# Expert lookups for eight tokens a visit, marks of 2048 elements, and three conditioning tiles moved

## The chip, the cores and the metric

The kernel runs on one core of one Trainium2 chip. The metric is the device time of one execution in microseconds (us); several runs of a kernel are taken, and their median counts. The engines are PE (matmuls; its weight loads are shown as PEld), DVE (elementwise and reductions), ACT (activations and copies), POOL, and SP, which here only issues DMA transfers. Each works through its own queue in order, and semaphores make one wait for another.

## What is computed

A chain of three transformer blocks on 256 tokens of width 1024: a first one with two attention mixers, a second one with two attentions and a gated feed-forward, and a third one that is conditioned on a vector c and ends in a mixture of many small experts. The change lies in the third, cut here to what matters:

```python
c_act = silu(c)
mod = c_act @ w_ada[l] + b_ada[l]            # 6 * 1024 conditioning values
shift1, scale1, gate1, shift2, scale2, gate2 = split(mod, 6)
h = modulate(x, norm_mix_g[l], shift1, scale1)
...                                          # pooling and attention, x = x + gate1 * ...
h2 = modulate(x, norm_ffn_g[l], shift2, scale2)
x = x + gate2 * peer_ffn(h2, ...)

def peer_ffn(h, w_q, sub_keys, u_tab, v_tab):
    # 8 heads: the 16 best of 128 keys on each of two sides, then the 16 best pairs:
    # expert = i * 128 + j out of 16384, with a softmax weight g
    u, vv = u_tab[expert], v_tab[expert]
    a = gelu(einsum('cd,chkd->chk', x, u))
    return einsum('chk,chkd->cd', g * a, vv)
```

## The kernel before

Activations are kept transposed, 128 features on the partitions and the 256 tokens along the row. Weights are streamed: `Weights` (lines 207 to 251) has one list of tiles of 128x1024 (512 KB), in the order in which they are used. A tile `wraw` is loaded by SP (L225, four buffers, three loads ahead). For precision it is split in two: `whi` by ACT (L242) and `wlo` by DVE (L243), and each projection step makes three matmuls, `whi` with the high part of the activations `hxh` (L460), `whi` with the low part `hxl` (L461), `wlo` with `hxh` (L462). There are three buffers for a split pair, and the split runs two tiles ahead of the matmuls.

The conditioning row `mod` is made on the side. Its 48 tiles of `w_ada` are put into the same list between others, at places given by the table `ADA`; such a tile is not split, but multiplied by silu(c) and summed along the row by one operation on DVE (L302, with a short read of the sum). So a conditioning tile costs one load in SP's queue, one of the four `wraw` buffers, and one place in DVE's queue. The names in the table are the weights after whose tiles they stand: `b2_ffn` the feed-forward of block two, `b3_v`, `b3_qk`, `b3_u`, `b3_g`, `b3_br` the values, queries and keys, pooling input, gates and branch products of block three, `pv` the experts' second table.

At the end of block two's feed-forward DVE makes `ft` from the gate (L1182, L1183), ACT and DVE split it into `fah` (L1186) and `fal` (L1187), PE multiplies by the last rows (L1173 to L1175) into the banks `s` and `t`, DVE adds to `xT` (L1047), and PE sums over `xT` (L431) for the norm. In block three attention is woven between the projections (`weave`, with a rate: so much of the side work for each step of the main work). A branch chunk's result in bank `pj` is taken over by DVE (L1329 `rx`, L1331 `sp`).

The experts (`peer`): routing finds each token's 128 pairs (i, j) and weights g. Then the products of all 16384 experts are made as a dense projection of 128 tiles (`u_evac`), and at the same time the table of weights `a[i, token]` is built from lookups (`combine`), woven in at the rate R_PEER. For one token a one-hot matrix of its keys i, times a one-hot matrix of its keys j scaled by g, gives a 128x128 table of weights: two matmuls of 128 columns (the weights g are in two parts of 16 bits). DVE makes the two matrices, called marks here: `ohx` (L1536, a comparison with a row of numbers) and `ohy` (L1539, `ohx` of the other key times g), for four tokens in one operation, two buffers each. One visit of PE (L1556) makes the eight matmuls of four tokens into one of the two PSUM banks `o`. Then DVE (L1566) and ACT (L1570) evacuate the bank: what of `a` already holds its product is multiplied by DVE, the rest is only written by ACT, and the later products are multiplied in by L1517. R_PEER, OHCOST and EVCOST say how much of this is due for each step of the projection. The final order of each engine's queue is set by the framework's scheduler from the order of writing.

## Time and profile before

| | us |
|---|---|
| median of three runs (1666.72 to 1670.72) | 1669.85 |
| the profiled execution, its own time | 1667.41 |
| its span, first to last instruction | 1665.6 |
| PE busy | 1618.2 (97%) |
| DVE busy | 1239.2 (74%) |
| ACT busy | 955.8 (57%) |
| first and last visit's lookups on PE | 981.3 and 1282.2 |

A row of a timeline gives the start, the duration, engine, line, operation, output and inputs with their shapes, a count of merged rows, and in brackets the idle time before it and who ended that. Matmuls overlap, so what a matmul costs is the distance between two starts, not the duration in its row. In a table of stretches each engine has its busy time in the stretch, with the number of instructions; PEclk is the granted share of TensorE's full clock.

### The profile page before, as it was taken

What the parts mean: (1) busy time and instruction counts of PE and PEld (TensorE: products, weight loads), DVE (VectorE), ACT (ScalarE), POOL (GpSimd) and SP (SyncE); (2) the same over time, 40 slices, a digit from 0 to 9 for tenths busy, and PEclk for the clock granted to TensorE, in tenths of its full rate; (3) what the DMA queues carried; (4) which work ended last, traced back from release to release, by engine and by line L of the source; (5) the groups of instructions that cost most, each with busy time, mean ns of one, the idle gap of its engine ahead of it and who ended that gap; (6) DMA issues with size and microseconds to landing.
All of it is one profiled execution on the core that took longest, in us unless ns stands there. A gap on an engine that the chain in (4) does not pass through costs nothing.

```text
span 1665.6 us, 30998 instructions
## 1 busy us (share of the span) xinstructions
PE 1618.2 (97%) x11828; PEld 1482.4 (89%) x11828; DVE 1239.2 (74%) x2502; ACT 955.8 (57%) x1810; POOL 182.1 (11%) x198
## 2 busy tenths in 40 slices
PE   9999999999999999999999999999999999999997
PEld 7999887788889999789989899999999888888886
DVE  6887888776776666787768987778887566666565
ACT  6775577568755555566555455555444655555554
POOL 2000234430120000111037000000000000000000
PEclk9999999999999999999999999999999999999999
DMA  7444552275247777447755555555555666666663
GB/s 253 146 138 149 170 184 79 84 226 161 90 129 252 245 236 254 150 143 228 259 160 169 164 190 172 170 165 172 168 168 170 199 222 213 214 213 209 185 195 115
DMA packets 84229, 300.07 MB, mean 180 GB/s; under 512 B 10288, under 2 KB 11184, under 8 KB 83824
## 3 DMA queue, kind: packets, MB, share of 16 engines
q1 hardware_dynamic: 83360, 295.90, 55.9%
q10 hardware_dynamic: 720, 2.19, 0.4%
q8 instruction: 93, 1.52, 0.4%
q14 instruction: 56, 0.46, 0.1%
HBM read 296.07 MB, written 1.05 MB: 178 GB/s over the span
## 4 chain that ended last, share of the span: by engine, by line
PE 69%; DVE 11%; DMA 7%; ACT 5%; issue 4%; POOL 1%; SPq 0%; POOLq 0%; DVEq 0%; ACTq 0%
PE s L1598 10%; PE t L1598 10%; PE pj L460 7%; PE pj L461 7%; PE pj L462 7%; DMA wraw<-in_ada 6%; DVE wlo L243 5%; PE s L460 3%; PE s L461 3%; PE t L460 3%; PE s L462 3%; PE t L461 3%; PE t L462 3%; PE o L607 2%; PE o L1556 2%
## 5 line engine op out<-in xcount | busy, mean ns | idle before, releaser
L242 ACT CAST whi<-wraw 128x1024 fp32r<-128x1024 f32 x504 | 528.9, 1051 | 356.0 <-PE pj L461 105.7
L243 DVE TENSOR_TENSOR wlo<-wraw,whi 128x1024 fp32r<-128x1024 f32 x486 | 598.9, 1238 | 172.8 <-ACT whi L242 170.7
L460 PE MATMUL pj<-hxh,whi 128*128 128x256 f32 x1448 | 412.1, 285 | 2.7 <-ACT hxh L1161 1.2
L461 PE MATMUL pj<-hxl,whi 128*128 128x256 f32 x1448 | 406.2, 281 | 1.3 <-DVE hxl L365 0.7
L462 PE MATMUL pj<-hxh,wlo 128*128 128x256 f32 x1448 | 406.1, 281 | 1.3 <-DVE wlo L243 0.8
L460 PEld LDWEIGHTS pj<-hxh,whi 128*128 128x128 f32 x1448 | 273.3, 189 | 10.4 <-issue 4.3
L461 PEld LDWEIGHTS pj<-hxl,whi 128*128 128x128 f32 x1448 | 272.6, 188 | 4.0 <-DVE hxl L1162 1.1
L462 PEld LDWEIGHTS pj<-hxh,wlo 128*128 128x128 f32 x1448 | 272.6, 188 | 3.4 <-DVE wlo L243 1.7
L1598 PE MATMUL s<-whi,hxl 128*128 128x512 f32 x512 | 157.9, 390 | 0.6 <-ACT hxl L1586 0.6
L1598 PE MATMUL t<-whi,hxl 128*128 128x512 f32 x512 | 157.6, 389 | 0.0
L1586 ACT CAST hxl<-a 128x256 fp32r<-128x256 f32 x128 | 51.8, 407 | 148.6 <-PE t L1598 146.8
L460 PE MATMUL s<-hxh,whi 128*128 128x256 f32 x456 | 129.7, 284 | 0.0
L462 PE MATMUL s<-hxh,wlo 128*128 128x256 f32 x456 | 127.7, 280 | 2.1 <-DVE wlo L243 2.1
L461 PE MATMUL s<-hxl,whi 128*128 128x256 f32 x456 | 127.6, 280 | 0.0
L460 PE MATMUL t<-hxh,whi 128*128 128x256 f32 x432 | 123.5, 286 | 1.6 <-ACT whi L242 1.6
L462 PE MATMUL t<-hxh,wlo 128*128 128x256 f32 x432 | 121.8, 282 | 1.4 <-DVE wlo L243 1.4
L461 PE MATMUL t<-hxl,whi 128*128 128x256 f32 x432 | 121.2, 281 | 0.0
L1598 PEld LDWEIGHTS s<-whi,hxl 128*128 128x128 f32 x512 | 95.9, 188 | 20.8 <-ACT hxl L1586 1.1
L1598 PEld LDWEIGHTS t<-whi,hxl 128*128 128x128 f32 x512 | 96.1, 188 | 20.0
L302 DVE SCALAR_TENSOR_TENSOR wraw<-wraw,cb 128x1024 f32<-128x1024 f32 x40 | 49.0, 1224 | 71.0 <-DMA wraw<-in_ada 71.0
L1587 DVE TENSOR_TENSOR hxl<-a,hxl 128x256 fp32r<-128x256 f32 x128 | 54.2, 424 | 57.8 <-PE t L1598 55.1
L462 PEld LDWEIGHTS s<-hxh,wlo 128*128 128x128 f32 x456 | 85.8, 188 | 2.7 <-DVE wlo L243 2.6
(398 smaller groups left out, 3226.7 us busy)
## 6 DMA issues: line engine op xcount, KB each, us to landing
wraw<-in_pu SPq DMA_DIRECT2D x128, 512.0 KB
wraw<-in_pv SPq DMA_DIRECT2D x128, 512.0 KB
wraw<-in_b_ffn SPq DMA_DIRECT2D x66, 512.0 KB
wraw<-in_ada SPq DMA_DIRECT2D x48, 512.0 KB
wraw<-in_b_qk SPq DMA_DIRECT2D x24, 512.0 KB
wraw<-in_fox_qk SPq DMA_DIRECT2D x16, 512.0 KB
wraw<-in_b_o SPq DMA_DIRECT2D x16, 512.0 KB
wraw<-in_b_g SPq DMA_DIRECT2D x16, 512.0 KB
```

Source lines behind the costliest of these rows:

```text
L242: nc.scalar.copy(hi, r)
L243: (nc.gpsimd if self.np in self.on_pool else nc.vector).tensor_tensor(lo, r, hi.bitcast(F32), op=OP.subtract)
L302: nc.vector.scalar_tensor_tensor(t, t, 1.0, cb, op0=OP.mult, op1=OP.mult, accum_out=modT[:, i:i + 1])
L460: nc.tensor.matmul(o, wh, xh, start=start, stop=False)
L461: nc.tensor.matmul(o, wh, xl, start=False, stop=False)
L462: nc.tensor.matmul(o, wl, xh, start=False, stop=stop)
L607: nc.tensor.matmul(o[a, kb * P:], v(e, kb), pts[e][:, kb * S:kb * P + S], start=start and not kb, stop=stop and kb == 1)
L1556: nc.tensor.matmul(p[:, t, :], x[:, w[0], :, w[1]], y[:, i, w[0], :, w[1]], start=i == 0 and t == 0, stop=i == 1, skip_group_check=True)
L1586: nc.scalar.copy(ah, src)
L1587: nc.vector.tensor_tensor(al, src, ah.bitcast(F32), op=OP.subtract)
L1598: nc.tensor.matmul(acc[tb][h], x[:, t], w[:, h * 512:h * 512 + 512], start=n == 0 and i == 0, stop=n == P - 1 and i == 2)
```

## The change

Marks are made for eight tokens in one operation of 2048 elements, with one buffer each in place of two of half the size. A visit makes 16 matmuls, eight into each of the two banks `o`; both banks are then evacuated (`use`, the same operations, now L1557 on DVE and L1561 on ACT), and the next marks are written after that. The rates that weave it in are set anew. Of the conditioning tiles, two go from behind the tiles 1 and 3 of `b3_v` to behind the tiles 1 and 3 of `b3_u`; the gates have seven, at other places, in place of six, and the branch products three in place of four.

```diff
-R_PEER, TOK, OHCOST, EVCOST = 0.35, 4, 1.4, 1.0
+R_PEER, TOK, OHCOST, EVCOST = 0.34, 8, 2.7, 0.9
...
-ADA = {"b2_qk": range(1, 16, 3), "b2_ffn": range(7, 64, 3), "b3_v": (1, 3), "b3_qk": range(1, 8, 2), "b3_g": (6, 8, 10, 12, 14, 15), "b3_br": range(1, 8, 2), "pv": range(16, 80, 8)}
+ADA = {"b2_qk": range(1, 16, 3), "b2_ffn": range(7, 64, 3), "b3_qk": range(1, 8, 2), "b3_u": (1, 3), "b3_g": (4, 6, 8, 10, 12, 13, 14), "b3_br": (1, 3, 6), "pv": range(16, 80, 8)}
...
-                    x, y = (hp.tile([P, 2, G, P, 2], F16, name=n, bufs=2) for n in ("ohx", "ohy"))
+                    x, y = (hp.tile([P, 2, G, P, 2], F16, name=n) for n in ("ohx", "ohy"))
...
-                for t0 in range(0, S, 4):
-                    x, y = oh[t0 // TOK]
-                    p = ps.tile([P, 4, P], F32, name="o")
-                    for t in range(4):
-                        w = (t0 % TOK + t) // 2, t % 2
-                        for i in range(2):
-                            nc.tensor.matmul(p[:, t, :], x[:, w[0], :, w[1]], y[:, i, w[0], :, w[1]], start=i == 0 and t == 0,
-                                             stop=i == 1, skip_group_check=True)
-                    if t0 % TOK == 0 and t0 + TOK < S:
-                        yield from made_of(t0 + TOK)
+                def use(t0, p):
                     u = made["u"]
...
                     made["t"] = t0 + 4
-                    yield EVCOST
+
+                for t0 in range(0, S, TOK):
+                    x, y = oh[t0 // TOK]
+                    ps_ = []
+                    for b in range(0, TOK, 4):
+                        p = ps.tile([P, 4, P], F32, name="o")
+                        for t in range(4):
+                            w = (b + t) // 2, t % 2
+                            for i in range(2):
+                                nc.tensor.matmul(p[:, t, :], x[:, w[0], :, w[1]], y[:, i, w[0], :, w[1]], start=i == 0 and t == 0,
+                                                 stop=i == 1, skip_group_check=True)
+                        ps_.append(p)
+                    for b, p in enumerate(ps_):
+                        use(t0 + 4 * b, p)
+                        yield EVCOST
+                    if t0 + TOK < S:
+                        yield from made_of(t0 + TOK)
```

The first place is DVE's queue at the end of block two's feed-forward; `fal` and `ft` are the parts of the gated product, `xT` takes the residual.

```order
 L243 TENSOR_TENSOR wlo<-wraw,whi 128x1024
 L1187 TENSOR_TENSOR fal<-ft,fah 128x256
-L302 SCALAR_TENSOR_TENSOR wraw,modT<-wraw,cb 128x1024
 L243 TENSOR_TENSOR wlo<-wraw,whi 128x1024
 L1182 TENSOR_TENSOR ft<-fg,o 128x256
@@ -921,5 +920,4 @@
 L243 TENSOR_TENSOR wlo<-wraw,whi 128x1024
 L1187 TENSOR_TENSOR fal<-ft,fah 128x256
-L302 SCALAR_TENSOR_TENSOR wraw,modT<-wraw,cb 128x1024
 L1047 SCALAR_TENSOR_TENSOR xT<-xT,s 128x256 x4
```

The two conditioning operations no longer stand ahead of the split and `ft`, nor ahead of the residual.

The second place is DVE's queue at the first branch products, before:

```order
L302 SCALAR_TENSOR_TENSOR wraw,modT<-wraw,cb 128x1024
L243 TENSOR_TENSOR wlo<-wraw,whi 128x1024
L1329 TENSOR_TENSOR rx<-pj,sg 128x512
L1331 TENSOR_TENSOR sp<-rx 128x256
L243 TENSOR_TENSOR wlo<-wraw,whi 128x1024
L365 TENSOR_TENSOR hxl<-sp,hxh 128x256
L302 SCALAR_TENSOR_TENSOR wraw,modT<-wraw,cb 128x1024
L1329 TENSOR_TENSOR rx<-pj,sg 128x512
L243 TENSOR_TENSOR wlo<-wraw,whi 128x1024
L1331 TENSOR_TENSOR sp<-rx 128x256
```

and after:

```order
L302 SCALAR_TENSOR_TENSOR wraw,modT<-wraw,cb 128x1024
L243 TENSOR_TENSOR wlo<-wraw,whi 128x1024
L1329 TENSOR_TENSOR rx<-pj,sg 128x512
L1331 TENSOR_TENSOR sp<-rx 128x256
L243 TENSOR_TENSOR wlo<-wraw,whi 128x1024
L365 TENSOR_TENSOR hxl<-sp,hxh 128x256
L1329 TENSOR_TENSOR rx<-pj,sg 128x512
L302 SCALAR_TENSOR_TENSOR wraw,modT<-wraw,cb 128x1024
L1331 TENSOR_TENSOR sp<-rx 128x256
L243 TENSOR_TENSOR wlo<-wraw,whi 128x1024
```

The second conditioning operation here comes behind the second `rx`, and it is the last one of the branch products' stretch, where one more followed before.

The third place is DVE's queue in the middle of the experts' stretch (the numbers behind `a` and `iota` only tell buffers apart), two visits before:

```order
L1566 SCALAR_TENSOR_TENSOR a_10627<-o,a_10627 128x64x4
L1566 SCALAR_TENSOR_TENSOR a_12216<-o,a_12216 128x4x4
L1536 TENSOR_TENSOR ohx<-iota_10631,keysT 128x1024
L1539 TENSOR_TENSOR ohy<-ohx,gT 128x1024
L243 TENSOR_TENSOR wlo<-wraw,whi 128x1024 x2
L1517 TENSOR_TENSOR a_12216<-a_12216,ux 128x120 x2
L1566 SCALAR_TENSOR_TENSOR a_10627<-o,a_10627 128x64x4
L1566 SCALAR_TENSOR_TENSOR a_12216<-o,a_12216 128x6x4
L1536 TENSOR_TENSOR ohx<-iota_10631,keysT 128x1024
L1539 TENSOR_TENSOR ohy<-ohx,gT 128x1024
L243 TENSOR_TENSOR wlo<-wraw,whi 128x1024
```

and one visit after:

```order
L1557 SCALAR_TENSOR_TENSOR a_10627<-o,a_10627 128x64x4
L1557 SCALAR_TENSOR_TENSOR a_12237<-o,a_12237 128x46x4
L1557 SCALAR_TENSOR_TENSOR a_10627<-o,a_10627 128x64x4
L1536 TENSOR_TENSOR ohx<-iota_10631,keysT 128x2048
L1539 TENSOR_TENSOR ohy<-ohx,gT 128x2048
L1517 TENSOR_TENSOR a_12237<-a_12237,ux 128x236 x2
L1557 SCALAR_TENSOR_TENSOR a_12237<-o,a_12237 128x48x4
L243 TENSOR_TENSOR wlo<-wraw,whi 128x1024 x3
L1517 TENSOR_TENSOR a_12237<-a_12237,ux 128x240 x2
L1557 SCALAR_TENSOR_TENSOR a_10627<-o,a_10627 128x64x4
```

The marks stand behind the evacuations of the visit before, and three splits stand between them and the next evacuation.

## Rows read from the trace of the kernel before

**Rows 1.** The page's busy times: us, share of the span, instructions.

```profile
PE 1618.2 (97%) x11828; PEld 1482.4 (89%) x11828; DVE 1239.2 (74%) x2502; ACT 955.8 (57%) x1810; POOL 182.1 (11%) x198
```

**Rows 2.** Stretches: length, then busy us of each engine, PEclk, DMA share, GB/s.

```profile
673.30:676.00 2.70, 2.70 (x15) 2.70 (x15) 1.84 (x5) 0.05 (x1) 0.00 (x0) 0.50 0.54 206
...
720.00:750.00 30.00, 28.40 (x211) 24.73 (x211) 28.46 (x83) 23.22 (x63) 2.58 (x2) 1.00 0.35 112
...
805.00:830.00 25.00, 22.82 (x192) 22.22 (x191) 23.49 (x40) 12.75 (x18) 0.00 (x0) 1.00 0.79 251
905.00:958.00 53.00, 49.53 (x419) 47.96 (x418) 52.09 (x227) 26.50 (x38) 6.83 (x3) 1.00 0.52 162
...
981.00:1284.00 303.00, 303.00 (x2836) 300.45 (x2835) 244.23 (x420) 152.94 (x380) 0.00 (x0) 1.00 0.54 169
```

**Rows 3.** PE's waits, two stretches: who waited for whom, total us, times, longest.

```profile
PE pj L460 <- DVE rx L1329: 2.0, 2, 1.5
...
PE s L462 <- DVE wlo L243: 2.1, 3, 1.0
PE pj L462 <- DVE wlo L243: 0.8, 2, 0.4
PE t L462 <- DVE wlo L243: 0.6, 2, 0.3
```

**Rows 4.** Timeline of PE around three visits.

```profile
1100.80 0.28 PE L462 MATMUL s<-hxh,wlo 128*128 128x256 f32 x1
1100.92 0.63 PE L1556 MATMUL o<-ohy,ohx 128*128 128x128 f16 x8
1101.36 0.37 PE L460 MATMUL s<-hxh,whi 128*128 128x256 f32 x1
1101.56 0.28 PE L461 MATMUL s<-hxl,whi 128*128 128x256 f32 x1
...
1105.21 0.28 PE L462 MATMUL t<-hxh,wlo 128*128 128x256 f32 x1
...
1105.57 0.28 PE L462 MATMUL t<-hxh,wlo 128*128 128x256 f32 x1
...
1115.74 0.28 PE L461 MATMUL pj<-hxl,whi 128*128 128x256 f32 x1
...
1119.61 0.28 PE L462 MATMUL s<-hxh,wlo 128*128 128x256 f32 x1
```

**Rows 5.** Timeline of DVE at the first of these visits.

```profile
1100.09 1.23 DVE L243 TENSOR_TENSOR wlo<-wraw,whi 128x1024 fp32r<-128x1024 f32 x1 [0.80 <-ACT whi L242]
...
1101.57 0.73 DVE L1566 SCALAR_TENSOR_TENSOR a<-o,a 128x248 f32<-128x248 f32 x2
1102.22 0.68 DVE L1536 TENSOR_TENSOR ohx<-iota,keysT 128x1024 f16<-128x1024 f16 x1
1102.93 0.69 DVE L1539 TENSOR_TENSOR ohy<-ohx,gT 128x1024 f16<-128x1024 f16 x1
```

**Rows 6.** Timeline of DVE at the end of block two's feed-forward.

```profile
667.27 1.23 DVE L302 SCALAR_TENSOR_TENSOR wraw<-wraw,cb 128x1024 f32<-128x1024 f32 x1 [2.16 <-DMA wraw<-in_ada]
...
669.56 0.41 DVE L1182 TENSOR_TENSOR ft<-fg,o 128x256 f32<-128x256 f32 x1
...
674.16 1.23 DVE L302 SCALAR_TENSOR_TENSOR wraw<-wraw,cb 128x1024 f32<-128x1024 f32 x1 [2.27 <-DMA wraw<-in_ada]
```

**Rows 7.** Timeline of PE in the same place.

```profile
669.74 0.28 PE L1175 MATMUL t<-fah,wlo 128*128 128x256 f32 x1
670.92 0.38 PE L1173 MATMUL s<-fah,whi 128*128 128x256 f32 x1 [0.90 <-ACT fah L1186]
...
675.93 0.66 PE L431 MATMUL o<-xT,mean__99 128*128 128x256 f32 x1
```

**Rows 8.** Timeline of DVE at the branch products.

```profile
805.64 1.23 DVE L302 SCALAR_TENSOR_TENSOR wraw<-wraw,cb 128x1024 f32<-128x1024 f32 x1 [1.16 <-DMA wraw<-in_ada]
...
811.30 1.23 DVE L302 SCALAR_TENSOR_TENSOR wraw<-wraw,cb 128x1024 f32<-128x1024 f32 x1 [0.77 <-DMA wraw<-in_ada]
```

## The prediction

> **What bounds the kernel now.** I read the page's busy shares first: PE is busy for 97% of the span [rows 1], so a gain has to be PE time, either time in which PE waits or time in which its matmuls follow each other more slowly than they could. The table of stretches comes next [rows 2]: in the experts' stretch (981 to 1284 us), where almost all edits of the change lie, PE is busy for all of 303.00 us and VectorE (DVE) for 244.23, while in four others PE stands: the end of block two's feed-forward (670 to 676, [rows 7]), the attention of block three (720 to 750, DVE 28.46 of 30 us), its branch products (805 to 830) and the routing (905 to 958, DVE 52.09 of 53). The list of PE's waits names whom it waits for [rows 3]. Last the timelines, for single steps [rows 4 to 8].
>
> In the experts' stretch PE waits for nobody, so whatever DVE saves there is worth nothing by itself. What PE pays is seen at a visit [rows 4]: the last projection matmul starts at 1100.80, the eight lookups take 0.44 us (1100.92 to 1101.36), and the second projection matmul after them starts at 1101.56. From 1100.80 to 1101.56 is 0.76 us for two projection matmuls and eight lookups. At an undisturbed step of 0.114 us (34 steps from 1115.74 to 1119.61) the two would take 0.23, so that 0.09 us is lost at the switch. There are 64 visits. The second thing in these rows is the step itself: 34 steps after one visit take 4.01 us (1101.56 to 1105.57, 0.118 each), 34 after another 3.87 (0.114). Going through all visits, the two steps alternate strictly: 32 of each, the fast one after the first, third, fifth visit and so on. The granted clock is 1.00 throughout [rows 2], so this is no clock level; no row names its cause.
>
> **The change, part by part.** The sum is made against the profiled execution: 1667.41 us, of which 1665.6 is the span. The median of the runs is 1669.85, 2.44 more; I take the differences over to the median.
>
> Visits: 32 instead of 64, each with 16 lookups in one row on PE. The lookups themselves stay (512). Saved: 32 x 0.09 = 2.9 us. Bounds: 0, if the change of bank in the middle of a visit costs what a switch costs, and 3.1. I take 2.9, since a bank change between projections (the names pj, s, t change every 48 matmuls) costs nothing in these rows.
>
> Marks: 128 operations of 1024 elements at 0.68 and 0.69 us [rows 5] become 64 of 2048, at most 1.38 us each. Cover: PE, which is busy throughout. The edit is priced at nothing, but its cover has to be looked at, because ohx and ohy now have one buffer. DVE may write the next marks only after PE has read the last, and PE's next visit waits for them. In the order after, ohx and ohy stand directly behind the evacuation of the visit before, or one split part (wlo) later, with two or three wlo between ohy and the next evacuation; so they are ready some 3 us early. Queued behind them on DVE is the next wlo, for which PE waits in its turn. A wlo that ended at 1101.32 was first needed at 1105.21 [rows 4, 5], 3.9 us later; the block of evacuations and marks on DVE grows by at most 1.7 us (one more evacuation, 0.36, and two marks longer by 0.69 each). Nothing is late: 0 us.
>
> [...]
>
> Routing: the rate of 0.34 for 0.35 spreads the same routing over 3% more projection matmuls. DVE is the bound there [rows 2], and PE waits 3.5 us for wlo (2.1, 0.8 and 0.6) [rows 3]. Half a weight chunk more of PE work (24 steps of 0.114, 1.4 us) comes with half a wlo of DVE work (0.6): 0.7 us saved; bounds -0.5 and 1.5.
>
> Feed-forward's end: two of the three moved conditioning tiles stood here, each a 512 KB load on SP's queue and an operation on DVE (L302). DVE is in order. The first L302 waited 2.16 us for its load and ended at 668.42; wlo and then ft (669.56) stood behind it [rows 6], and PE waited for what ACT makes of ft [rows 7]. [...] From 669.74 to 675.93 it made 25 steps in 6.19 us, against 25 x 0.114 = 2.85. With both L302 gone DVE gets 2.16 + 1.15 = 3.3 us back ahead of ft, more than PE's first wait (670.92 - 669.74 - 0.11 = 1.1) needs; the second (waited 2.27 until 674.16) held the residual adds and would be late next, and goes too. I take the whole 3.3 us. Bounds: 0, if wlo waits for its own input there anyway, and 3.3. Past this the sums over xT follow PE's last matmuls and move with them; SP's queue reaches block three's first weights two loads earlier.
>
> Block three's attention: the two tiles come in here (b3_u). 1.23 us each on a DVE that is busy 28.46 of 30 us [rows 2, 6]. In the order after, one stands among the softmaxes, the other at their end, where the load on DVE falls. DVE had been late with its weights here, so the tiles' loads have long landed. I add 1.2 us, one of the two; bounds 0 and 2.5.
>
> Branch products: four tiles become three, and one more goes into the gates before (where PE stands nowhere). PE waits twice, together 2.0 us, for rx [rows 3], both times with an L302 ahead of it on DVE that had waited for its load (1.16 and 0.77) [rows 8]. In the order after, no L302 stands between the first and the second rx, and the one ahead of the first is loaded one slot earlier. I take 2.2 us, the waits with the slow first steps behind them; bounds 0 and 2.6.
>
> Sum: -2.9 - 0.7 - 3.3 + 1.2 - 2.2 = -7.9. 1667.41 - 7.9 = 1659.5 for an execution like the profiled one; as a median, 1669.85 - 7.9 = **1662.0 us** (0.47% faster).
>
> **Rivals.** What the sum leaves out is the step after a visit. My forecast lets it go on as a mixture of both, as now.
>
> All fast: there is one kind of visit now, so there may be one kind of step. If it is the fast one, 32 stretches of 35 steps gain 0.004 each, 4.5 us: 1657.5. For it: behind most interruptions elsewhere the fast step comes back.
>
> All slow: the same 4.5 us lost, 1666.5. For it: each visit now ends on the second of the two banks, and it was after visits to the second that the step was slow.
>
> Slower than before: the marks set the pace. DVE has 244.23 us of 303.00 [rows 2], 7.6 us in the 9.4 of two old visits; without the four marks (2.74) 4.9. With two marks of m us it becomes the bound at 4.9 + 2m = 9.4, m = 2.2. The marks would reach that if the wider operation lost its pace: at twice the 1.23 us of the 32-bit wlo [rows 5], m = 2.46, PE stands 0.4 to 0.45 us in each of 32 visits, some 14 us: 1676. Against it: 1024 16-bit elements take 0.69 where 32-bit ones take 1.23, and the inner shape of the operation stays.
>
> The change doesn't do what it says: the loss at a visit goes with its lookups or banks rather than with the visit, and the waits at the feed-forward's end and the branches have other releasers. Then 2.9, and most of 5.5, are gone: 1669.
>
> Fewer, larger operations pay by themselves: 64 operations less on DVE. From 0.69 us for 1024 elements, if half were fixed, 64 x 0.34 = 22 us less DVE time, of which PE could see no more than it waits; in the experts' stretch it waits for nothing, so no less than 1661 comes out. [...]
>
> **How the numbers follow.** Chances: forecast 0.37, all fast 0.27, all slow 0.22, slower 0.08, not as it says 0.04, fewer operations 0.02. About 0.3%, 5 us, is what a measurement can tell from no change: 1664.8 and 1674.9 are the borders. Faster: nearly all of all fast and fewer operations (0.28), 0.28 of the forecast's 0.37 (bounds of the terms), 0.05 of all slow: 0.61. Slower: 0.07 and 0.01 of the rest, 0.08. The same: 0.31. The range takes all fast with its terms at their best (1656) and all slow with the two wait terms half gone (1669.5), and leaves out the slower rival and a rest, 0.2 in all.
>
> **What would show it.** Visits: 32 rows of sixteen lookups (or two of eight) with one switch of about 0.09 us; the time from the first visit to the last. The step: 35 steps after a visit at 0.114 or 0.118. The feed-forward's end: no wait of PE for fah, no stretch at clock 0.50 before the sums, and 3 us earlier there. Branches: no wait for rx. Attention: an L302 among the softmaxes, and who waits behind it. Marks: 1.2 to 1.4 us. The prediction is wrong if PE waits for ohy, wlo or a bank in the experts' stretch, or if the waits that I take away come back a few us later.

## The result and the profile after

The changed kernel took 1658.56 us (median of three runs, 1658.43 to 1658.83) against 1669.85, a ratio of 0.9936 with an interval of 0.9922 to 0.9949: about 0.6% faster. The forecast was 1662.0, in a range of 1656.0 to 1669.5. The profiled execution took 1658.43 us, its span 1656.7, which is 8.9 less than the span before; the sum had said 7.9. Part of the 11.3 us between the medians is the draw of three runs: beside the experiments the kernel before ran 72 more times, with medians of 1667.11, 1667.66, 1667.53 and 1665.75 in four groups. Beside those the gain is some 7 to 9 us.

The total hides that the parts did not come as forecast. The page's busy times of after, as [rows 1], and the stretches that answer to [rows 2] (length, busy us of PE, PEld, DVE, ACT and POOL with instructions, PEclk, DMA share, GB/s):

```profile
PE 1607.8 (97%) x11828; PEld 1473.9 (89%) x11828; DVE 1231.9 (74%) x2435; ACT 957.9 (58%) x1804; POOL 177.8 (11%) x198
```

```profile
666.00:672.00 6.00, 6.00 (x54) 6.00 (x54) 4.29 (x8) 3.25 (x5) 0.00 (x0) 1.00 0.71 239
716.00:746.00 30.00, 26.98 (x200) 23.62 (x199) 28.17 (x80) 22.01 (x59) 2.59 (x2) 1.00 0.39 129
801.00:826.00 25.00, 22.32 (x195) 21.96 (x194) 21.10 (x35) 13.26 (x18) 0.00 (x0) 1.00 0.77 248
...
980.00:1280.00 300.00, 300.00 (x2876) 298.85 (x2875) 238.80 (x358) 157.87 (x381) 0.00 (x0) 1.00 0.56 173
```

The end of the feed-forward (first row) now has PE busy throughout at a granted clock of 1.00, where [rows 2] had 0.50; it stays at 1.00 up to the sums over `xT`, which begin at 672.82. In the attention (second row) PE is busy for less than before, 26.98 of 30 us. In the experts (last row) PE is busy throughout, as before, but issues 2876 instructions in 300 us where it issued 2836 in 303.

Five distances between landmarks on PE say where the time went. They are used for all experiments below:

- feed-forward: from the first sum of squares ahead of block two's feed-forward (L441) to the first of the next norm (L400)
- attention: from the first L594 of block three to the pooling's first product (L1273)
- gates: from there to the first branch product (the first L460 that reads the pooling's result, `pph`); branches: from there to the next norm's first sum (L399)
- experts: from the end of the matmul ahead of the routing's second long wait for `wlo` (950.31 in before) to the end of the one ahead of the output projection's wait for `hxl` (1308.55)

| kernel | feed-forward | attention | gates | branches | experts | ratio to before |
|---|---|---|---|---|---|---|
| before | 208.5 | 45.0 | 30.0 | 49.0 | 358.2 | |
| after | 205.1 | 49.5 | 29.1 | 47.9 | 350.6 | 0.9936 |
| e1, experts' part only | 206.7 | 45.0 | 30.0 | 47.8 | 350.0 | 0.9963 |
| e2, tiles only | 205.1 | 48.5 | 30.7 | 48.0 | 357.5 | 0.9994 |
| e3, one buffer of marks | 209.0 | 45.0 | 30.0 | 48.6 | 357.5 | 1.0001 |
| e4, one bank | 209.5 | 45.0 | 30.0 | 48.0 | 361.4 | 1.0025 |
| e5, marks of 2048 | 208.6 | 45.0 | 30.0 | 49.2 | 357.5 | 0.9998 |
| e6, visits of 16 lookups | 210.7 | 45.0 | 30.0 | 50.4 | 350.0 | 0.9947 |
| e7, tiles in the feed-forward | 215.0 | 45.0 | 30.0 | 46.3 | 350.0 | 0.9963 |
| e8, one short visit | 211.4 | 45.0 | 30.0 | 48.1 | 351.0 | 0.9960 |
| e9, two tiles to b3_u | 205.5 | 47.6 | 30.1 | 47.6 | 358.2 | single run |
| e10, tiles in block two | 205.3 | 45.0 | 30.0 | 46.3 | 350.0 | 0.9945 |
| e11, visits of 4 to 16 | 209.4 | 45.0 | 30.0 | 48.7 | 355.5 | single run |
| e12, tiles spread | 205.2 | 45.1 | 30.0 | 46.0 | 349.9 | 0.9934 |

Before to after: feed-forward -3.4, attention and gates +3.5, branches -1.1, experts -7.6, the rest -0.3. So the experts hold nearly the whole gain. The three conditioning tiles give about as much as they take: 3.4 at the feed-forward's end for 4.4 in the attention. The 0.9 of the gates and the 1.1 of the branches have another source, shown under e8 and e11.

What a visit looks like now, as [rows 4]: timeline of PE in after around one visit of sixteen lookups and up to the next.

```profile
1101.72 0.28 PE L462 MATMUL t<-hxh,wlo 128*128 128x256 f32 x1
1101.84 1.09 PE L1572 MATMUL o<-ohy,ohx 128*128 128x128 f16 x16
1102.74 0.36 PE L460 MATMUL t<-hxh,whi 128*128 128x256 f32 x1
1102.94 0.28 PE L461 MATMUL t<-hxl,whi 128*128 128x256 f32 x1
...
1111.57 0.28 PE L462 MATMUL pj<-hxh,wlo 128*128 128x256 f32 x1
```

From 1101.72 to 1102.94 is 1.22 us for two projection matmuls and sixteen lookups; two old visits took 2 x 0.76 for four projection matmuls and as many lookups. With the projections taken off at 0.114, that is 0.99 for 1.06, so 0.07 saved per new visit, 2.2 us for 32. The 76 steps from 1102.94 to 1111.57 take 8.63 us, 0.1136 each: the faster of the two old steps. It stands so behind all 32 visits. In before 32 stretches of some 34 steps had 0.118, so 32 x 34 x 0.0042 = 4.6 us are saved there. 2.2 and 4.6 are 6.8 of the 7.6.

DVE at the same visit, as [rows 5]:

```profile
1103.87 0.75 DVE L1557 SCALAR_TENSOR_TENSOR a<-o,a 128x256 f32<-128x256 f32 x2
1104.53 1.21 DVE L1536 TENSOR_TENSOR ohx<-iota,keysT 128x2048 f16<-128x2048 f16 x1
1105.78 1.23 DVE L1539 TENSOR_TENSOR ohy<-ohx,gT 128x2048 f16<-128x2048 f16 x1
1106.92 1.22 DVE L243 TENSOR_TENSOR wlo<-wraw,whi 128x1024 fp32r<-128x1024 f32 x1
```

Marks of 2048 take 1.21 and 1.23 us where 1024 took 0.68 and 0.69 [rows 5], and are ready at 1107.0, 4.7 us ahead of the next visit at 1111.69. If an operation's time is a fixed part and one in proportion to its elements, the fixed part is 2 x 0.685 - 1.22 = 0.15 us, an estimate from these two sizes. PE got nothing of it, as e5 shows (0.9998).

PE's waits in after between 700 and 830 us (who waited for whom, total us, times, longest):

```profile
PE pj L460 <- DVE rx L1329: 2.7, 2, 2.0
PE t L1273 <- DVE win L1267: 1.9, 1, 1.9
PE s L555 <- ACT str L544: 1.4, 1, 1.4
PE o L607 <- DVE ptw L598: 1.0, 1, 1.0
PE t L594 <- DVE pn L588: 0.9, 1, 0.9
PE pj L462 <- DVE wlo L243: 0.7, 1, 0.7
```

The first was 2.0 in before [rows 3] and was to go. The second, fourth, fifth and sixth are new: 1.9 + 1.0 + 0.9 + 0.7 = 4.5, which is what the attention lost (49.5 for 45.0).

### The profile page after: what moved, and what is told of

Read it like the earlier page. It is cut to its first block, busy times and chain, and to the rows that moved or that the text cites. A ratio compares the mean times of both kernels' runs of the same rounds, so it can differ in the third digit from the quotient of the medians.

```text
span 1656.7 us, 30936 instructions
## 1 busy us (share of the span) xinstructions
PE 1607.8 (97%) x11828; PEld 1473.9 (89%) x11828; DVE 1231.9 (74%) x2435; ACT 957.9 (58%) x1804; POOL 177.8 (11%) x198
## 4 chain that ended last, share of the span: by engine, by line
PE 76%; DVE 9%; ACT 4%; DMA 3%; issue 3%; POOL 1%; SPq 0%; POOLq 0%; DVEq 0%; ACTq 0%
PE s L1605 10%; PE t L1605 10%; PE pj L460 7%; PE pj L461 7%; PE pj L462 7%; DVE wlo L243 3%; PE s L460 3%; PE s L461 3%; PE s L462 3%; PE t L460 3%; PE t L461 3%; PE t L462 3%; DMA wraw<-in_ada 2%; PE o L1572 2%; PE o L607 2%
## 5 line engine op out<-in xcount | busy, mean ns | idle before, releaser
L460 PE MATMUL pj<-hxh,whi 128*128 128x256 f32 x1448 | 410.2, 284 | 2.7 <-ACT hxh L1161 1.2
L460 PEld LDWEIGHTS pj<-hxh,whi 128*128 128x128 f32 x1448 | 272.7, 188 | 9.9 <-issue 3.9
L460 PE MATMUL s<-hxh,whi 128*128 128x256 f32 x456 | 128.0, 281 | 0.0
L460 PE MATMUL t<-hxh,whi 128*128 128x256 f32 x432 | 121.8, 282 | 0.9 <-ACT whi L242 0.9
L302 DVE SCALAR_TENSOR_TENSOR wraw<-wraw,cb 128x1024 f32<-128x1024 f32 x40 | 48.9, 1223 | 67.3 <-DMA wraw<-in_ada 67.3
```

The costliest lines, as they stand in the source:

```text
L302: nc.vector.scalar_tensor_tensor(t, t, 1.0, cb, op0=OP.mult, op1=OP.mult, accum_out=modT[:, i:i + 1])
L460: nc.tensor.matmul(o, wh, xh, start=start, stop=False)
```

## The experiments

### e1 and e2: the two halves of the change

e1 is after with the old table, e2 is before with the new one:

```diff
-ADA = {"b2_qk": range(1, 16, 3), "b2_ffn": range(7, 64, 3), "b3_v": (1, 3), "b3_qk": range(1, 8, 2), "b3_g": (6, 8, 10, 12, 14, 15), "b3_br": range(1, 8, 2), "pv": range(16, 80, 8)}
+ADA = {"b2_qk": range(1, 16, 3), "b2_ffn": range(7, 64, 3), "b3_qk": range(1, 8, 2), "b3_u": (1, 3), "b3_g": (4, 6, 8, 10, 12, 13, 14), "b3_br": (1, 3, 6), "pv": range(16, 80, 8)}
```

> The experts' part of the change alone; the conditioning tiles stand as before. My theory after the result: the visits (32 x 0.09 = 2.9 us) and the fast step after every visit (32 intervals at 0.1137 for 0.1178, 4.6 us) make 7.5 us in the experts' stretch, and the three moved tiles the remaining 1.4: so 7.5 us below before in the span, 0.9955 of it, and no slow step after any visit. Rival: the step after a visit depends on what happened earlier (where the matmul stream stood when the experts' stretch began), and the moved tiles turned it: then only 2.9 us below before, and steps that alternate or are all slow.

> The kernel before with the three moved conditioning tiles alone. My theory: 3.7 us earlier at the end of block two's feed-forward, of which block three's attention, gates and branch products give back 2.3, so 1.4 us below before at the routing and at the end (0.999 of it); the steps after the visits alternate as before. Rival: the tiles carry more than that, because the gain that block three gives back depends on the experts' part too: 3 us or more below before at the end. By the prediction's terms it would be 4.3.

e1: 0.9963, interval 0.9948 to 0.9978; the experts take 350.0 us and every step behind a visit is the fast one. e2: 0.9994, interval 0.9978 to 1.0011, which is no difference; the feed-forward takes 205.1, the attention 48.5, the experts 357.5 with steps in turn. Both as the theory had it: the gain is the experts', and the tiles come to about nothing. The two ratios make 0.9957 together where that of the whole change is 0.9936; the intervals allow the difference, and no stage shows it. The span of e1's profile (1650.1) is shorter than that of after, but 3.6 us of that were gained ahead of block two's feed-forward, where the two kernels do not differ, so it says nothing on the tiles; the stages do.

### e3 and e4: what sets the step

One buffer for the marks (e3), one bank for all visits (e4):

```diff
-                    x, y = (hp.tile([P, 2, G, P, 2], F16, name=n, bufs=2) for n in ("ohx", "ohy"))
+                    x, y = (hp.tile([P, 2, G, P, 2], F16, name=n) for n in ("ohx", "ohy"))
```

```diff
+                p = ps.tile([P, 4, P], F32, name="o")
                 for t0 in range(0, S, 4):
                     x, y = oh[t0 // TOK]
-                    p = ps.tile([P, 4, P], F32, name="o")
```

> The kernel before with one buffer for ohx and ohy instead of two; 64 visits of eight lookups, banks in turn, marks of 1024, as before. Three theories on the two steps (0.114 and 0.118 us) that followed the visits in turn. If it was the buffer of marks that a visit read, all 64 intervals have one step now (all 0.114: 4.6 us less). If it was the bank that a visit filled, or if each run of eight lookups turns the step over, they alternate as before and nothing is saved. Should PE have to wait for the marks, rows that wait for DVE stand ahead of lookups, at most 1.4 us each.

> The kernel before with one bank for all 64 visits; ohx and ohy keep two buffers in turn. If the bank that a visit filled sets the step, all intervals have one step. If the buffer of marks sets it, or each run of eight lookups turns it over, they alternate (0.114 and 0.118) as before. The visits stand at uneven distances here (20 to 50 steps of 0.114 for 32 to 44), since a visit waits for the evacuation of the one before: PE may wait some tenths of a us at some of them, which says nothing on the theories.

e3: 1.0001 (0.9985 to 1.0017). The steps go in turn, as in before, and begin with 0.118 behind the first visit where before began with 0.114. The buffer of marks does not set the step, and neither does the place in the row of visits, since the first visit of two kernels with the same order left different steps.

e4: 1.0025 (1.0012 to 1.0039), the experts 361.4 us. Both steps are still there with one bank, so the bank does not set them. Where PE had stood ahead of a visit, as at 22 of the 64 here, the fast step came behind it each time. Timeline of PE in e4 at such a visit:

```profile
999.99 0.28 PE L462 MATMUL pj<-hxh,wlo 128*128 128x256 f32 x1
1000.49 0.62 PE L1556 MATMUL o<-ohy,ohx 128*128 128x128 f16 x8 [0.22 <-ACT a L1570]
1000.91 0.36 PE L460 MATMUL pj<-hxh,whi 128*128 128x256 f32 x1
1001.11 0.28 PE L461 MATMUL pj<-hxl,whi 128*128 128x256 f32 x1
```

The lookups start 0.50 us after the last projection matmul, where 0.12 is usual, since ACT still reads the bank. One bank costs 3.2 to 3.9 us in the experts, 361.4 for 358.2 in before and 357.5 in e3. To fill both banks in one visit cost PE no wait: after has none between 980 and 1280 us.

### e5 and e6: marks or visits

e5 has marks of 2048 in one buffer but visits of eight lookups; e6 has visits of 16 in two banks but marks of 1024 in two buffers. The loops, cut:

```diff
-R_PEER, TOK, OHCOST, EVCOST = 0.35, 4, 1.4, 1.0
+R_PEER, TOK, OHCOST, EVCOST = 0.35, 8, 0.2, 2.3
...
+                for t0 in range(0, S, TOK):
+                    x, y = oh[t0 // TOK]
+                    for b in range(0, TOK, 4):
+                        p = ps.tile([P, 4, P], F32, name="o")
...
+                        if b + 4 == TOK and t0 + TOK < S:
+                            yield from made_of(t0 + TOK)
+                        use(t0 + b, p)
+                        yield EVCOST
```

```diff
+                yield from made_of(0)
+                yield from made_of(4)
+                starts = list(range(0, S, 8))
+                for v, t0 in enumerate(starts):
...
+                    for t1, p in ps_:
+                        use(t1, p)
+                        yield EVCOST
+                    for t1 in range(len(oh) * 4, min(end + 8, S), 4):
+                        yield from made_of(t1)
```

> The kernel before with marks of 2048 in one buffer, as after, but still 64 visits of eight lookups. What counts is the time from the second wait of the routing (943 to 950 us) to the start of the output projection: 357.5 to 358.2 us in the kernel before and in the two variants that kept 64 visits, 350.0 to 350.6 with 32. Theory now: the gain belongs to the visits alone, so 357.5 to 358.2 here too, steps of 0.114 and 0.118 in turn, and a time within 0.2% of before. Rival: the wider marks save PE something; then below 356.

> The kernel before with 32 visits of 16 lookups into both banks, but marks of 1024 in two buffers, as before; the conditioning tiles stand as before. Theory: all of the experts' gain is here: 350.0 to 350.6 us from the routing's second wait to the output projection, 0.114 after every visit, 7.5 us less than before (0.9955). Rival: the marks of 2048 are needed for it (DVE's 64 operations, or one buffer read by every visit): then 355 us and steps that alternate.

e5: 0.9998 (0.9987 to 1.0009), experts 357.5. e6: 0.9947 (0.9929 to 0.9964), experts 350.0. Everything that the experts gained is the longer visit's, and the marks of 2048, half the operations on DVE, bring PE nothing.

### e8 and e11: when does the slow step come

e8 is e6 with `starts = [0, *range(4, S, 8)]`, e11 has `sizes` of 2, 4, 6 and 8 tokens, that is 4 to 16 lookups, in a random order in place of equal visits.

> As the one with 32 visits of 16 lookups and marks of 1024, but with a single visit of eight at the start (and so one of eight at the end). Theory: each run of eight lookups turns the step over, so a visit of 16 brings it back to where it was; in the kernel before the two steps followed in turn, and with 16 the step stayed at the fast one because it was so at the start. Then a single visit of eight turns it once, and nearly all of the 31 intervals behind it have the slow step: 0.118, 4.6 us more than with 32 equal visits (355 us from the routing's second wait to the output projection for 350.3). Rival: a visit of 16 that fills both banks always leaves the fast step; then 350.5. Third: the change of phase at the start differs from run to run, and neither holds.

> The kernel before with visits of 4, 8, 12 and 16 lookups in a random order (61 of them), marks of 1024 in two buffers; some visits stand so near that PE may wait for marks, which is not looked at. Read is the step (0.114 or 0.118) in an interval of 14 steps or more, by the length of the visit ahead and the step before it. Known so far: eight lookups turn the step over either way; sixteen left the fast one after either. Theory: up to eight a visit turns it, from some length on it always leaves the fast one; 4 as 8, 12 as 16. Rival: each eight lookups turn it by themselves, so that 4 and 12 leave an irregular picture; or there is no rule by length, and 8 lookups leave either step here too.

e8 (0.9960, 0.9946 to 0.9975) took 351.0 us in the experts, so the theory that each eight lookups turn the step over fell. Timeline of PE in e8 at its first two visits:

```profile
983.40 0.63 PE L1575 MATMUL o<-ohy,ohx 128*128 128x128 f16 x8
983.84 0.37 PE L460 MATMUL pj<-hxh,whi 128*128 128x256 f32 x1
984.04 0.28 PE L461 MATMUL pj<-hxl,whi 128*128 128x256 f32 x1
...
988.05 0.28 PE L462 MATMUL s<-hxh,wlo 128*128 128x256 f32 x1
988.17 1.09 PE L1575 MATMUL o<-ohy,ohx 128*128 128x128 f16 x16
```

The 34 steps from 984.04 to 988.05 take 4.01 us, 0.118 each, behind the visit of eight. Behind the visit of sixteen at 988.17, and behind all others of sixteen, the step is 0.1136 or 0.1137.

e11 gives the whole picture, read from its timeline (stretches of fewer than 12 steps left out):

| lookups in the visit | step before it 0.114 | step before it 0.118 |
|---|---|---|
| 4, 12, 16 | 0.114 behind each | 0.114 behind each |
| 8 | 0.118 behind each of 14 | 0.114 behind each of 5 |

The theory held for 8, 12 and 16 lookups and fell for 4, which act as 12 do. So behind a visit the slow step belongs to one case, a run of exactly eight lookups (of the four lengths tried) that comes while the stream runs at the fast step. The other kernels with visits of eight, read in the same way, agree: of 202 such visits that met the fast step without a wait of PE, 201 left the slow one, and all 179 that met the slow step left the fast one. The one exception is the first visit of before. In the kernel before all 64 visits were of that length, and every second one left the slow step. e11 has 61 visits and still needs 355.5 us for 358.2. Why eight, is open: buffers, banks and the marks' size are ruled out, and no row names a cause.

The slow step is not confined to visits, though. The same 25 us in the gates' products, first before, then after (columns as in [rows 2]):

```profile
775.00:800.00 25.00, 25.00 (x215) 25.00 (x214) 14.78 (x21) 17.08 (x27) 0.00 (x0) 1.00 0.77 260
```

```profile
775.00:800.00 25.00, 25.00 (x223) 25.00 (x223) 16.10 (x22) 18.05 (x29) 0.00 (x0) 1.00 0.78 253
```

And the timeline of PE in the branch products, again before and after:

```profile
821.97 0.28 PE L461 MATMUL pj<-ppl,whi 128*128 128x256 f32 x1
...
850.00 0.28 PE L462 MATMUL t<-hxh,wlo 128*128 128x256 f32 x1
```

```profile
816.10 0.28 PE L461 MATMUL pj<-ppl,whi 128*128 128x256 f32 x1
...
848.53 0.28 PE L462 MATMUL t<-hxh,wlo 128*128 128x256 f32 x1
```

In all four PE waits for nothing. Before makes 215 matmuls in the gates' 25 us and after 223; in the branches 238 steps take 28.03 us in before, 0.118 each, and 286 take 32.43 us in after, 0.113 each. Over the whole stages the slow step stands at 238 of 253 recorded steps of the gates in before and at none in after, and at 284 of 379 in the branches in before and at 3 of 381 in after. At 0.0043 us a step that is an estimate of 1.0 and 1.2 us, as much as the 0.9 and 1.1 by which the two stages became shorter. No lookups stand near, kernels with the same code in the branches differ in it (27 slow steps in e4, 285 in e5), and what brings it there was not tried. Within the experts it explains why kernels with the same visits differ: before has it in all 178 recorded steps behind the last visit (358.2 where e3 has 357.5), after in some 200 steps ahead of the first (350.6 where e1 has 350.0).

### e9: the tiles in block three's attention

Before, with `"b3_v": (1, 3)` replaced by `"b3_u": (1, 3)` and nothing else.

> The kernel before with two conditioning tiles moved from block three's values to its attention inputs (b3_u), and gates and branch products as before. In the runs so far the stretch from the end of the feed-forward to the first wait in block three's attention took the same in all; the next one, up to the pooling's transposes, took 45.0 us where the tiles stood in b3_v or in the feed-forward, and 48.5 and 49.5 with all three edits; the branch products 47.8 to 50.4 with four tiles and 47.9 with three. Theory: the two tiles in b3_u are the whole of it: 48.5 to 49.5 here too, 205.1 for the feed-forward (206.7 to 211.4 with the old places), and 47.8 to 50.4 for the branches. Rival: the tile that comes in earlier in the gates holds the pooling: then 46 to 47.5 here, and the remaining 2 belong to the gates' edit.

A single run took 1662.64 us beside a median of 1667.53. Feed-forward 205.5, attention 47.6, branches 47.6. The attention lies between the two theories, so both edits take part: the two tiles in b3_u cost 2.6 us, and the gates' new places bring it to 48.5 in e2 and 49.5 in after. These two have the same table; the last 1.0 is PE's wait for `ptw`, which e2 lacks, and why is not shown. How it comes to PE's wait of 1.9 us for `win` in after is seen in the chain of work that ended last, in order of time (start us, us, what; `in_b_g` is the gates' weights):

```profile
746.57 5.55 DMA wraw<-in_b_g
...
758.28 4.70 DMA wraw<-in_b_g
763.08 1.06 ACT whi L242
764.16 0.98 DVE wlo L243
...
765.30 1.14 DVE wraw L302
766.53 0.88 DVE win L1263
767.52 1.29 POOL win L1260
...
772.59 0.23 DVE win L1267
772.86 1.99 PE t L1273 x8
```

The gates' weights come late, DVE splits them late, then stands an L302, and only behind it the second of the pooling's sums (L1263), from which POOL and DVE go on in turn up to L1267. In before the chain from 740 to 780 us is PE's own work but for 2.1 us; that sum began at 764.41, and L1273 waited for nothing. That the weights are late because each tile ahead of them holds one of the four `wraw` buffers until DVE reads it fits the code, but was not tried by itself.

### e7, e10 and e12: other places for the tiles

All three are after with another table; b3_v, b3_u and (but for one tile in e12) the branches have none:

```diff
+ADA = {"b2_qk": range(1, 16, 3), "b2_ffn": sorted([*range(7, 64, 3), 12, 18, 24, 30, 36, 42]), "b3_qk": range(1, 8, 2), "b3_g": (6, 8, 10, 12, 14, 15), "pv": range(16, 80, 8)}
...
+ADA = {"b2_qk": range(1, 14, 2), "b2_o": (1, 3, 5, 7), "b2_ffn": range(7, 64, 3), "b3_qk": range(1, 8, 2), "b3_g": (6, 8, 10, 12, 14, 15), "pv": range(16, 80, 8)}
...
+ADA = {"b2_qk": (1, 2, 3, 4, 5, 7, 9, 11, 13), "b2_ffn": range(7, 64, 3), "b3_qk": range(1, 8, 2), "b3_g": (6, 8, 10, 12, 13, 14, 15), "b3_br": (1,), "pv": range(16, 80, 8)}
```

> The changed kernel with six conditioning tiles more in the middle of block two's feed-forward (DVE 26 of 40 us there) and none in block three's values, attention inputs (b3_u) or branch products; the gates have six again. Theory: what block three gave back (3.5 us between the end of the feed-forward and the end of block three, against the kernels with the old places) was an L302 ahead of a chain that PE waited for; without it the end of the feed-forward keeps its 3.4 us, the attention and the gates cost what they cost before, and the waits for rx go (about 2 us). So 5 us below after, 0.997 of it, and 0.991 of before. Rival: DVE is late in block three whatever stands ahead (its load is 28 of 30 us in the attention), the waits move to the next releaser, and the gain is 1 us or less; or the feed-forward, which moves 236 to 251 GB/s, waits for its weights, and PE stands between 500 and 650 us.

> The changed kernel with the moved tiles where block two's attention runs (two in b2_qk, four in b2_o; the transfers keep 0.36 to 0.46 of the DMA engines busy there, against 0.7 in the feed-forward), none in block three's values, b3_u or branches, six in the gates. Theory: the place of a tile costs what stands behind its transfer on DVE; here DVE is busy for 15 to 16 of 20 us and the transfers have room, so that block two's attention grows by no more than 2 us, the feed-forward takes 205.1 us, block three's attention 45.0 and the branches 46.4 (as with the tiles in the middle of the feed-forward). Then 5 us or so below after, 0.991 of before. Rival: each tile costs PE about 1.6 us wherever it stands, as in the middle of the feed-forward (8 us for five waits there): then no better than after.

> The changed kernel with the conditioning tiles where no chain that PE waits for stands behind them on DVE: four more early in b2_qk (nine for five, ahead of and between the first softmaxes of block two, none in the later ones), none in block three's values or b3_u, seven in the gates from the seventh weight chunk on, one in the branches. Theory: the place decides. Block two's feed-forward 205.1 us, block three's attention up to the pooling 45.0, gates 30.0, branches 46.4 to 47, and block two's attention at most 1 us longer than before (176.8 from the first score of its values to the feed-forward's first product), where the four tiles in b2_o cost 2.6 with two L302 among the late softmaxes. Then some 4 us below after: 1654 to 1655, 0.991 to 0.992 of before. Rival: each tile in block two's attention costs PE some 0.6 us wherever it stands: 179 there, and no better than after (0.9936).

In block three all three did what was expected: attention 45.0 or 45.1, branches 46.0 to 46.3. But each paid elsewhere, and beside the kernel before none reached the 0.991 or 0.992 that was expected. e7 (0.9963, 0.9951 to 0.9975): 215.0 in the feed-forward. DVE there, and PE:

```profile
546.95 1.22 DVE L302 SCALAR_TENSOR_TENSOR wraw<-wraw,cb 128x1024 f32<-128x1024 f32 x1 [2.67 <-DMA wraw<-in_ada]
548.10 0.08 DVE L302 DVE_READ_ACCUMULATOR wraw<-wraw,cb 128x1 f32 x1
548.10 0.42 DVE L1187 TENSOR_TENSOR fal<-ft,fah 128x256 fp32r<-128x256 f32 x1
```

```profile
548.57 0.39 PE L1174 MATMUL s<-fal,whi 128*128 128x256 f32 x1 [1.56 <-DVE fal L1187]
```

The operation waits 2.67 us for its transfer with `fal` behind it; PE waited 8.4 us for `fal` between 490 and 660 us, 2.4 in before. DVE is busy for only 25 to 27 of 40 us there (520 to 560), and that is no measure of room: in before the whole 14.7 us of its idle time in these 40 us lies ahead of L302, in front of the queue.

e10 (0.9945, 0.9928 to 0.9961): from block two's L934 wait to the feed-forward's first wait 179.4 us, where the kernels with five tiles there take 175.6 to 176.9; two L302 stand among the softmaxes, and PE waits 2.8 us for `pn` on two rows where it waited 1.1. e12 (0.9934, 0.9918 to 0.9949) avoids these and takes 178.7, with one wait of 2.55 us at another place. DVE in e12, and PE:

```profile
374.05 1.22 DVE L302 SCALAR_TENSOR_TENSOR wraw<-wraw,cb 128x1024 f32<-128x1024 f32 x1 [1.72 <-DMA wraw<-in_ada]
...
376.33 0.68 DVE L1081 TENSOR_TENSOR qk<-pj,rqk 128x512 f32<-128x512 f32 x1
377.13 1.22 DVE L302 SCALAR_TENSOR_TENSOR wraw<-wraw,cb 128x1024 f32<-128x1024 f32 x1
...
378.40 0.42 DVE L546 TENSOR_TENSOR str<-qk,str 64x256 fp32r<-64x256 f32 x1
```

```profile
378.96 0.55 PE L555 MATMUL s<-stc,str 128*128 128x256 f32 x1 [2.55 <-ACT stc L545]
```

The product that waits reads `stc` and `str`, which ACT and DVE make from `qk`, and `qk` stands on DVE behind the L302 that waited 1.72 us for its transfer. By the stages e12 is 5.4 us better than after in block three and 1.8 worse in block two (178.7 for 176.9); by the times, 0.9934 against 0.9936, the two cannot be told apart. No version clearly better than after was found.

## Why the forecast held, and where it was wrong

The sign and the size came out: 1658.56 in the range, 8.9 us between the profiles for 7.9. But errors of nearly 7 us either way cancelled. The faster step gave 4.6 us behind the visits and, by the estimate above, some 2 in the gates and branches, all of which the sum had left out. Against that the attention (3.2), the branches (2.2), the routing (0.7) and the visits (0.7) gave less than it took. So the size came out by luck, and for other reasons than the sum gave.

**Visits**, -2.9: right in kind, 2.2 by the rows, a little less, since the switch costs 0.11 rather than 0.09 where sixteen lookups stand in a row (1.22 - 0.23 - 0.88).

**The step**, priced at 0, as a mixture of both: wrong. "All fast", the first rival, is what happened, 4.6 us. The prediction named evidence on both sides but forecast the case that had none, that one kind of visit would leave two steps. That the last bank decides, its reason for "all slow", fell with after itself, whose visits all end on the second bank, and with e4. It could not have been settled from the trace of before, where all visits have eight lookups; and the reason given for "all fast", that elsewhere the fast step mostly comes back, passed over the gates and branches of before, which run at the slow one for most of their length.

**Marks**, 0: right; no wait in the experts, and e5 shows 0. The rival on which the marks set the pace had them at 2.46 us where 1.21 came. "Fewer, larger operations" fell with e5.

**Routing**, -0.7: wrong. From the norm's first sum (L399) to the routing's second wait it takes 100.0 us for 100.1, and 100.0 to 100.1 in e1 and e2. The term took the weave's rate for a distance on the chip; the waits for `wlo` there hardly moved (3.2 us for 3.5).

**Feed-forward's end**, -3.3: right, -3.4; both waits and the stretch at clock 0.50 are gone. Beside the mean of the old places it is 4.1. The kernels with the old places take 206.7 to 211.4 us, eight profiles with a mean of 209.2, and those without an L302 there 205.1 to 205.5 (e7 apart, whose tiles stand in its middle).

**Attention**, +1.2: mis-sized, +4.4. The step that failed is "one of the two": both tiles are paid for (waits of 0.9, 0.7 and 1.0 us), on a DVE that is busy 28 of 30 us. "The tiles' loads have long landed" was true of the tiles and overlooked the weights behind them, which the chain of after now runs over. And the gates' seventh tile, priced at nothing because PE stands nowhere in the gates, acts ahead of them: loads and splits run ahead of their place in the list, so that three L302 stand ahead of the pooling's last steps (760.11, 765.30, 770.18) for one in before (763.26). PE's wait there is 1.9 us; e9, without the gates' edit, has 0.6 of it.

**Gates**, priced at nothing: -0.9 in the stage, from the faster step alone.

**Branches**, -2.2: failed. The stage's -1.1 is the faster step's (1.2 by the estimate above), and the waits for rx, which were to go, are 2.7 for 2.0. Kernels with the old places there have 1.7 (e9) to 3.1 (e6) and e2 with the new ones 1.8, so that the edit of the branches shows no effect either way. The prediction saw that no L302 stood between the first and the second rx any more, and stopped there. It stands behind the second now, ahead of `sp`, from which the third follows. DVE in after:

```profile
805.20 1.23 DVE L302 SCALAR_TENSOR_TENSOR wraw<-wraw,cb 128x1024 f32<-128x1024 f32 x1 [1.63 <-DMA wraw<-in_ada]
...
810.01 0.68 DVE L1329 TENSOR_TENSOR rx<-pj,sg 128x512 f32<-128x512 f32 x1
812.12 1.23 DVE L302 SCALAR_TENSOR_TENSOR wraw<-wraw,cb 128x1024 f32<-128x1024 f32 x1 [1.42 <-DMA wraw<-in_ada]
813.27 0.08 DVE L302 DVE_READ_ACCUMULATOR wraw<-wraw,cb 128x1 f32 x1
813.27 0.42 DVE L1331 TENSOR_TENSOR sp<-rx 128x256 f32<-128x256 f32 x1
...
815.08 0.68 DVE L1329 TENSOR_TENSOR rx<-pj,sg 128x512 f32<-128x512 f32 x1
```

`sp` needs only the rx that ended at 810.7 and starts at 813.27, and the third rx comes behind it at 815.08. PE's fifth group of products waits 1.96 us for that rx. That the waits go when the tiles go is shown by e7 and e10, with none in the branches: no row for rx among PE's waits, and 46.3.

## What to carry to other kernels

An operation that waits for a transfer was a block in the road here: in e7 `fal` stood on DVE behind an L302 that waited 2.67 us, and PE waited 1.56 us for `fal`. Moving the tiles removed one wait and made the next, 3.4 us gained at the feed-forward's end for 4.4 lost in the attention, so follow the whole chain behind the new place of such an operation, and look where its place in the queue is, not in the list of weights. DVE's idle time was no room for it: the 14.7 us from 520 to 560 us in before were themselves spent waiting for the transfers, and with six more tiles in the feed-forward e7 took 215.0 us there for 205.1 in after. Where a short burst of another kind of matmul interrupts a long stream, measure the stream's step behind the burst for two or three lengths of it: here eight lookups left a slower step behind every second visit of before (0.118 us for 0.114) and sixteen behind none of the 32 of after, which was worth more (4.6 us) than the interruptions saved (2.2). And read the step in the stages that an edit does not touch as well: the gates became 0.9 us shorter with no wait removed.

## What the runs showed of the hardware

The stream of 128x256 matmuls, each with its weight load, ran at one of two steps, 0.114 or 0.118 us, both at a granted clock of 1.00. It kept one for the 28 to 76 steps between two visits of before or after, and for more than 200 in the gates and branches. Runs of 4, 12 or 16 matmuls of 128 columns left the fast one (each one of e11, and the 32 of after); runs of eight left the slow one if the fast one was running (201 of 202), and the fast one otherwise (179 of 179), or where PE had stood ahead of them (22 of 22 in e4). What brings the slow one away from the visits is open.

The marks, 16-bit operations on DVE, took 1.22 us for 2048 elements and 0.685 for 1024: by a line through these two, an estimate, 0.15 fixed and 0.53 for each 1024. A lookup of 128 columns took 0.055 us in a row of eight (0.44 in before) and 0.056 in a row of sixteen (0.90 in after).

The same instructions on the same data took up to 4.7 us more or less in the feed-forward (206.7 to 211.4, in eight profiles) as long as operations that wait for transfers stood in DVE's queue at its end, and 205.1 to 205.5 without them, in five profiles.
